# One transformer layer on one core: the last projection's first blocks by seven products, and the order around the second norm

## The chip, the cores and the metric

The program runs on one core of one Trainium2 chip. A core has four engines that this document speaks of: TensorE (PE, matrix products into eight banks of PSUM of 128 x 512 words each), VectorE (DVE), ScalarE (ACT) and SyncE (SP, which here issues loads and stores). Each takes its instructions in its own fixed order and waits on semaphores for the others. The metric is the device time of one launch in microseconds (us), smaller is better. Batch is 1, 512 tokens (S), model width 1024 (D), FFN width 2816, all in float32.

## The reference

The layer mixes the tokens in three branches, merges them and ends with a gated FFN. Only the end matters here; everything ahead of it is unchanged.

```python
    x = x + rms_norm(merged @ w_o, g_post_mix)

    hf = rms_norm(x, g_pre_ffn)
    f_gate, f_up = jnp.split(hf @ w_ffn_in, 2, axis=-1)
    f = (jax.nn.silu(f_gate) * f_up) @ w_ffn_out
    return x + rms_norm(f, g_post_ffn)
```

The last line but one's product with w_ffn_out (2816 x 1024) is the "last projection". The first two lines hold two norms: the one of merged @ w_o (its sum of squares is the first sum below) and the one of the new x (the second sum); the normed rows are then transposed to feed the FFN.

## The kernel before, in words

**Two halves of a number.** A product of two float32 matrices is made from three products of float32r operands: each operand is split into a high part (ScalarE copies it, line L119) and a low part (VectorE subtracts, L124), and TensorE adds high x high, high x low and low x high. So every operand costs ScalarE and VectorE one pass each, and each product block three matmuls. `split` at L118 does it.

**Weights.** A table `wlist` (L129 to L170) names every 128 x 1024 piece of weights in the order of its use. `unit()` hands out the next one and sees to it by `wload` that the two behind it are loaded by SP into one of two buffers `raw` and split into one of three buffers `hi` and `lo`. A tag in the table sends a unit's halves to a buffer of another pool (named u), which is how more of them can lie ready at the kernel's end.

**The two norms (`wo_norm`, L1039).** The 512 tokens are four blocks of 128, done as two pairs: `wo_norm(0)` and, later, `wo_norm(2)`, the "second norm" of this document. For each of four 128 x 512 half rows ScalarE squares with a sum (junk, L1047) and VectorE multiplies with the gain (yg, L1049). Then VectorE adds the sums (ss, L1051), makes an inverse root in twelve steps on 128 x 2 words (L273 to L279), updates x in four operations (xr, L1058), for which ScalarE squares again (L1060); a second sum (L1062) and inverse root, four multiplications (xn, L1070); TensorE transposes each in four pieces (tr, L1075); ScalarE copies (xf, L1081) and both split into fh and fl.

**The FFN's head (`ffn_head`, L1108).** The first three pairs of row blocks (six units of w_ffn_in, gate and up) run on all 512 tokens by plain products: `passes` (L221), first the six units over the first 256 tokens (fh, fl of `wo_norm(0)`), 144 matmuls of 128x256, then the same units over the others. `wo_norm(2)` runs beside them: its steps are handed out between matmuls, and a number of empty steps (L1064) sets before which matmul of the head its transposes stand. Behind it `begin_pairs` (L1154) prepares the first pair of the next stage: sums of token blocks (`make`), their splits (`halve`), and `pair_prep` (L1214 on), which sums and splits weight blocks.

**The pairs (`pairs`, L1248).** The other 19 of the 22 row blocks of gate and up go by seven products instead of eight (a 2 x 2 block scheme; product names s1 to s4, a11, a12, a22; `product` is L1250 with its matmul at L1254, z, y, r1 to r3 are its banks and partial results, rawp the raw weights of two buffers). Each product is 12 matmuls of 128x256. The result, silu(gate) x up, is stored as 22 slabs f of 128 x 512.

**The last projection (`down`, L1307).** It takes f by 11 units (pairs of row blocks, 256 rows of w_ffn_out by 512 columns each, per column half). `down(0, 0)` makes the first 512 columns of all tokens in four banks, one per token block, then `down(1, 4)` the others: `block` (L1322) does 6 matmuls of 128x512 at L1328. f is split (`f_split`, L1099) as the units of the first half come. `close` squares a bank with a sum and multiplies by the gain; with both halves' sums it makes the root, scales, adds x and stores. Units of the second half's last four are kept together, so that the four token blocks end one after the other and only the last is closed behind the last matmul.

The order of work is that of the code as written, except that a scheduler may exchange independent instructions between engines' queues, and `tc.issue_after(X)` keeps an instruction behind X in the order without a wait.

## Time and profile before

| what | value |
|---|---|
| median of 3 runs (lowest, highest) | 1130.61 us (1129.9, 1132.03) |
| the profiled execution's own time | 1130.71 us |
| its span (first to last instruction) | 1129.0 us |
| TensorE, share of the span | 99%, 6212 matmuls |
| VectorE, ScalarE | 70%, 53% |
| granted TensorE clock, mean | 0.999 |
| span of the FFN's head (771.43 to 811.14) | 39.71 us |
| span of the pairs (811.14 to 1000.33) | 189.19 us |
| last projection to the last matmul (1000.33 to 1121.79) | 121.46 us |
| behind the last matmul | 7.21 us |

The times in the trace count from the start of the span. The profiled execution is one launch; its own time is 0.10 us over the median. Busy times of matmuls overlap, since the next one starts before the last has ended; "x4" behind an operation of a timeline means four of them drawn together as one row. A bracket at the end of a timeline row is the idle time ahead of it and what ended it.

### The profile page before, as it was taken

The numbers are of one execution on the slowest core, as the hardware profiler recorded it, in microseconds if no ns is written. First come the engines' busy times: TensorE is split into PE (matmuls) and PEld (weight loads), VectorE is DVE, ScalarE is ACT, GpSimd is POOL, SyncE is SP. The second block draws the span as 40 slices with busy tenths as digits, with TensorE's granted clock in tenths as the row PEclk, the third lists the DMA queues.
The fourth block names the chain that finished last, engine by engine and source line by source line (L and its number), as shares of the span: only waits on it lengthen the run. The fifth ranks groups of instructions, "written<-read, shape, count | busy, mean of one in ns | idle before, by whom it ended". The sixth has DMA issues, their size and how long they took to land.

```text
span 1129.0 us, 15949 instructions
## 1 busy us (share of the span) xinstructions
PE 1117.4 (99%) x6212; PEld 965.6 (86%) x6212; DVE 790.4 (70%) x1425; ACT 599.1 (53%) x1077; POOL 23.2 (2%) x39
## 2 busy tenths in 40 slices
PE   9999999999999999999999999999999999999997
PEld 8888778888889888888888888888999999998886
DVE  6966967262675899999998644558887878882333
ACT  6757674132344786767776533334655555671221
POOL 1000202100000000000000000000000000000000
PEclk9999999999999999999999999999999999999999
DMA  8332325323232211111111252522233323323332
GB/s 307 111 93 75 112 94 204 95 75 102 84 94 76 75 38 56 38 57 57 38 58 56 74 204 94 150 85 65 75 112 110 101 90 113 113 94 98 107 94 75
DMA packets 29868, 108.74 MB, mean 96 GB/s; under 512 B 3232, under 2 KB 3520, under 8 KB 28640
## 3 DMA queue, kind: packets, MB, share of 16 engines
q1 hardware_dynamic: 27344, 97.98, 27.1%
q10 hardware_dynamic: 2160, 9.04, 2.2%
q8 instruction: 49, 0.80, 0.3%
q0 software_dynamic: 288, 0.69, 0.2%
q14 instruction: 27, 0.22, 0.1%
HBM read 105.60 MB, written 2.10 MB: 95 GB/s over the span
## 4 chain that ended last, share of the span: by engine, by line
PE 94%; DVE 3%; ACT 1%; DMA 1%; issue 0%; DVEq 0%; ACTq 0%
PE mm L221 42%; PE mm L1254 17%; PE mm L1328 11%; PE mm L507 4%; PE o L857 4%; PE mm L1032 3%; PE sc L819 3%; PE tr L844 3%; PE mm L735 2%; PE tr L651 1%; PE tr L433 1%; DMA rawp<-in_w_fi 1%; PE tr L567 1%; PE tr L757 1%; DVE lo L124 1%; PE mm L290 0%
## 5 line engine op out<-in xcount | busy, mean ns | idle before, releaser
L119 ACT ACTIVATE hi<-raw 128x1024 fp32r<-128x1024 f32 (+1 forms) x124 | 130.4, 1051 | 212.1 <-PE mm L221 86.2
L124 DVE TENSOR_TENSOR lo<-raw,hi 128x1024 fp32r<-128x1024 f32 (+1 forms) x124 | 151.4, 1221 | 128.5 <-ACT hi L119 121.4
L221 PE MATMUL mm<-hh,hi 128*128 128x512 f32 x504 | 199.9, 397 | 0.0
L221 PE MATMUL mm<-hh,lo 128*128 128x512 f32 x504 | 197.5, 392 | 0.2 <-DVE lo L124 0.2
L221 PE MATMUL mm<-hl,hi 128*128 128x512 f32 x504 | 197.2, 391 | 0.0
L221 PEld LDWEIGHTS mm<-hh,lo 128*128 128x128 f32 x504 | 94.6, 188 | 20.0 <-DVE lo L124 0.5
L221 PEld LDWEIGHTS mm<-hh,hi 128*128 128x128 f32 x504 | 94.7, 188 | 18.8 <-ACT hi L119 0.4
L221 PEld LDWEIGHTS mm<-hl,hi 128*128 128x128 f32 x504 | 94.7, 188 | 18.5 <-issue 0.2
L825 ACT ACTIVATE P<-P,ast 128x128 f32<-128x128 f32 (+3 forms) x128 | 70.6, 554 | 23.1 <-DVE ast L823 22.5
L1328 PE MATMUL mm<-hi,fs 128*128 128x512 f32 x256 | 79.8, 389 | 0.0
L823 DVE CUSTOM_DVE_ANT_0 P<-sc,mask 128x128 f32<-128x128 f32 (+3 forms) x128 | 57.9, 484 | 8.2 <-PE sc L819 7.3
L119 ACT ACTIVATE ph<-tr 128x512 fp32r<-128x512 f32 x80 | 47.0, 593 | 29.2 <-PE tr L844 28.3
L124 DVE TENSOR_TENSOR pl<-tr,ph 128x512 fp32r<-128x512 f32 x80 | 54.3, 684 | 5.1 <-ACT ph L119 3.2
L1328 PEld LDWEIGHTS mm<-hi,fs 128*128 128x128 f32 x256 | 48.1, 188 | 10.0
L819 PE MATMUL sc<-K,q 128*128 128x512 f32 (+2 forms) x192 | 50.9, 367 | 0.0
L1328 PE MATMUL mm<-lo,fs 128*128 128x512 f32 x128 | 49.8, 389 | 0.0
L1254 PE MATMUL mm<-t,hi 128*128 128x256 f32 x264 | 48.9, 283 | 0.0
L844 PE MATMUL tr<-ident,P 128*128 128x128 f32 x320 | 48.7, 273 | 0.0
L844 PEld LDWEIGHTS tr<-ident,P 128*128 128x128 f32 x320 | 39.1, 140 | 9.8 <-DVE pl L124 0.9
L1254 PEld LDWEIGHTS mm<-t,hi 128*128 128x128 f32 x264 | 41.1, 192 | 0.0
L1254 PE MATMUL mm<-fh,u 128*128 128x256 f32 x192 | 38.5, 283 | 0.0
L1254 PE MATMUL mm<-t,u 128*128 128x256 f32 x288 | 38.4, 283 | 0.0
(355 smaller groups left out, 2596.6 us busy)
## 6 DMA issues: line engine op xcount, KB each, us to landing
raw<-in_w_in SPq DMA_DIRECT2D x64, 512.0 KB, 3.6
rawp<-in_w_fi SPq DMA_DIRECT2D x19, 1024.0 KB, 5.0
raw<-in_w_br SPq DMA_DIRECT2D x24, 512.0 KB, 3.5
raw<-in_w_fo SPq DMA_DIRECT2D x22, 512.0 KB, 3.6
w<-in_cw ACTq DMA_DIRECT2D x4, 1024.0 KB, 6.8
raw<-in_w_o SPq DMA_DIRECT2D x8, 512.0 KB, 3.6
raw<-in_w_v SPq DMA_DIRECT2D x7, 512.0 KB, 5.1
raw<-in_w_fi SPq DMA_DIRECT2D x6, 512.0 KB, 3.6
```

What stands on the lines that cost most here:

```text
L119: SC.activation(hi, src, AF.Copy)
L124: res["lo"] = V.tensor_sub(lo, src, f32(hi))
L221: res["mm"] = PE.matmul(ps[:m, n0:n1], w[:, k * 128:k * 128 + m], x[k][:, n0:n1], start=(t == 0), stop=(t == 3 * NK - 1))
L507: res["mm"] = PE.matmul(b[c], x[k][:, c * 128:(c + 1) * 128], w[:, kk * 512:kk * 512 + 512], start=(k == 0 and t == 0), stop=(k == NK - 1 ...
L819: PE.matmul(ps[:, :w * n].rearrange("p (b n) -> p b n", b=w), lhs, K[:, i, brs[0]:brs[-1] + 1, :n], start=(i == 0), stop=(i == 1))
L823: V.tensor_tensor_reduce(out=t, in0=ps[:, b * n:b * n + n], in1=mask[0][:, S - n:], scale=-0.125, scalar=3.0e38, op0=OP.add, op1=OP.min, a ...
L825: SC.activation(t, t, AF.Exp, scale=-1.0, bias=st[:, 0, j, b:b + 1], accum_out=st[:, 1, j, b:b + 1])
L844: PE.transpose(pt[:, j * 128:(j + 1) * 128], self.part(j, br)[:, kt * 128:(kt + 1) * 128], ident)
L857: PE.matmul(po, VV[:, kt, g % 2, br].rearrange("p i d -> p (i d)"), x, start=(br == 0 and kt == 0 and t == 0), stop=(br == 1 and kt == a a ...
L1032: res["mm"] = PE.matmul(b[c, f], x[k][:, q], w[:, fs], start=(k == 0 and t == 0), stop=(k == NK - 1 and t == 2))
L1254: PE.matmul(ps, w[:, k * 128:k * 128 + 128], x[:, k], start=(start and k == t == 0), stop=(k == 3 and t == 2), skip_group_check=True)
L1328: PE.matmul(b[c], x[k][:, q], w[:, ws], start=(k == 0 and t == 0), stop=(k == NFF - 1 and t == 2))
```

## The change

**Last projection.** The first 4 of the 11 pairs of row blocks are multiplied in another way. Within two pairs of row blocks (one slab f of four row blocks), the operands are cut in 2 x 2: A by token half (256 tokens) and by even or odd row block, B by even or odd row block and by column half. The eight block products of such a matrix product are replaced by seven (1 to 7) of sums and differences: s1 to s4 of A (on VectorE, in the place of f), t1 to t4 of B (on VectorE, in the place of the loaded weights bs). Both slabs (q = 0, 1) go into the same banks, so a product is two halves of 12 matmuls, 128x512 each. `prep` splits the two operands of one half, A into one of four half buffers of u (which the pairs stage uses up to its end), B into the hi and lo buffers of the units. The other 7 pairs stay plain: `plain` is four `block`s. All eight banks hold partial results: w, x, y, z are two each. They are copied (s1, s5, early) or added between products, and `close` adds the copy first, where it has one (s). The raw weights of the four pairs are now loaded by four loads of 1 MB, whole slabs bs.

**Second norm.** The squares at L1047 are issued behind fh's last split of the first norm (`fhi`); the empty steps ahead of the transposes are 12 instead of 14; the steps of `begin_pairs` are issued behind xr (the first) or xn (the others) instead of yg.

```diff
-    HEAD, LAST, LASTV = 3, 4, 2
+    HEAD, LASTV = 3, 2
...
-    wlist += [(A["w_fo"][i], "y" if 22 - LAST <= i < 20 else None) for i in range(22)]
+    NS, NP = 4, NFF // 2
+    fo = {}
+    wlist += [(A["w_fo"][NP + i], None) for i in range(NS, 2 * NS)]
+    for n in (1, 2, 5, 6, 3, 7, 4):
+        if n == 4:
+            wlist.append((A["w_fo"][NP + 2 * NS], None))
+        wlist += [((n, q), None) for q in range(2)]
...
+            if isinstance(ap, tuple):
+                hi = wts.tile([128, 1024], F32R, tag="hi", name=nm("hi"), bufs=3)
+                lo = wts.tile([128, 1024], F32R, tag="lo", name=nm("lo"), bufs=3)
+                fo["prep"](*ap, hi, lo)
...
-                SC.activation(j, b[c, f], AF.Square, scale=0.5, accum_out=ss[:, f, c:c + 1])
+                with tc.issue_after(res["fhi"].ins) if "fhi" in res else nullcontext():
+                    SC.activation(j, b[c, f], AF.Square, scale=0.5, accum_out=ss[:, f, c:c + 1])
...
-        for _ in range({0: 8, 2: 14}[c0]):
+        for _ in range({0: 8, 2: 12}[c0]):
...
-        def step():
-            with tc.issue_after(res["yg"].ins):
+        def step(ins=res["xn"].ins):
+            with tc.issue_after(ins), tc.issue_after(res["fhi"].ins):
                 next(prep)
-        step()
+        step(res["xr"].ins)
...
+        misc = slab("misc", tag="y", shape=(2, 2, S))
+        fo["bs"] = [[slab("bs", tag="mo", shape=(2, 2, S)) for _ in range(2)] for _ in range(2)]
+        for h in range(2):
+            for q in range(2):
+                SY.dma_start(fo["bs"][h][q].rearrange("p u k n -> p u (k n)"),
+                             A["w_fo"][NP * h + 2 * q:NP * h + 2 * q + 2].rearrange("u p n -> p u n"))
...
+        def prep(n, q, hi, lo):
+            a, b = {1: ("a11", "b11"), 2: ("a12", "b21"), 5: ("s1", "b11"), 6: ("a11", "b11"), 3: ("a12", "b22"),
+                    7: ("a21", "b12"), 4: ("a22", "b21")}[n]
+            e = fo["n"] % 4
+            fo["n"] += 1
+            u = ff["unit"][e // 2][:, e % 2].rearrange("p (l i t) -> p l i t", l=2, i=2)
+            fo["a"][n, q] = u[:, 0], u[:, 1]
+            split(fo[a, q], u[:, 0], u[:, 1])
+            split(fo[b, q], *(t.rearrange("p (i n) -> p i n", i=2) for t in (hi, lo)))
...
+                d, x, y, op = {"s1": ("s1", "a21", "a22", OP.add), "s3": ("a21", "a11", "a21", OP.subtract),
+                               "s2": ("a11", "s1", "a11", OP.subtract), "s4": ("a12", "a12", "a11", OP.subtract),
+                               "t1": ("b11", "b12", "b11", OP.subtract), "t2": ("b11", "b22", "b11", OP.subtract),
+                               "t3": ("b12", "b22", "b12", OP.subtract), "t4": ("b21", "b21", "b11", OP.subtract)}[name[:2]]
+                V.tensor_tensor(g(d), g(x), g(y), op=op)
...
+        def product(n, q):
+            ps = {1: z, 6: z, 7: z, 4: z, 2: y, 5: w, 3: w}[n]
+            bh, bl = unit()
+            ah, al = fo["a"].pop((n, q))
+            for i in range(2):
+                f = slice(512 * i, 512 * i + 512)
+                for m in range(2):
+                    t = slice(128 * m, 128 * m + 128)
+                    mac(ps[m], (ah[:, i, t], bh[:, f]), (ah[:, i, t], bl[:, f]), (al[:, i, t], bh[:, f]))
...
+            ps, s = {(0, 0): (y, s1), (0, 1): (w, fo["early"]), (1, 0): (z, None), (1, 1): (x, s5)}[c // 2, h]
...
+        plain(1, NS)
...
+        plain(1, NS + 3)
+        fo_sum("s21", "t10")
+        product(1, 0)
+        fo_sum("t11")
+        product(1, 1)
+        for m in range(2):
+            SC.activation(fo["early"][m], w[m], AF.Copy)
+            begun.discard(id(w[m]))
+        product(2, 0)
+        product(2, 1)
...
+        for i in range(NS, NS + 3):
+            plain(0, i)
+        us = [unit() for _ in range(4)]
+        for c in range(4):
+            for i in range(4):
+                block(0, c, NS + 3 + i, *us[i])
+            close(0, c)
...
-    run([down(0, 0), down(1, LAST)])
+    down()
```

Left out are the buffers' tags, the rest of the products' order (2, 5, 6, 3, 7, a plain unit, 4, two plain units, the closing of the second column half), and the renaming of y in `close`.

What this does to the order of the instructions is shown at three places. **ScalarE at the second norm**, before: xf and fh are the last copies and splits of the first norm, junk at L1047 the squares of the second, a22h and hi belong to the preparation of the pairs.

```order
L1081 ACTIVATE xf_1128_6604<-tr_1132_6632 128x4x128 [waits PE_49]
L119 ACTIVATE fh_1016_5837<-xf_1128_6604 128x4x128 [waits Activation_49]
L1047 ACTIVATE junk_1138_6674,ss_5836<-mm_1105_6462 128x512 [waits PE_49]
L119 ACTIVATE a22h_1197_7023<-rawp_1160_6765 128x512 [waits DMAHW0_49]
L1081 ACTIVATE xf_1128_6604<-tr_1134_6648 128x4x128 [waits PE_49]
L1047 ACTIVATE junk_1140_6678,ss_5836<-mm_1106_6463 128x512 [waits DVE_49]
L119 ACTIVATE fh_1017_5838<-xf_1128_6604 128x4x128 [waits Activation_49]
L1047 ACTIVATE junk_1142_6682,ss_5836<-mm_1107_6464 128x512 [waits DVE_49,PE_49]
L1047 ACTIVATE junk_1144_6686,ss_5836<-mm_1108_6465 128x512 [waits DVE_49,PE_49]
L119 ACTIVATE hi_1189_6974<-rawp_1160_6765 128x1024 [waits DVE_49]
```

And after (the line numbers are those of the changed kernel; L1099 is the copy xf, L1065 the first squares, L1078 the second):

```order
L1099 ACTIVATE xf_1128_6604<-tr_1132_6632 128x4x128 [waits PE_49]
L119 ACTIVATE fh_1016_5837<-xf_1128_6604 128x4x128 [waits Activation_49]
L1099 ACTIVATE xf_1128_6604<-tr_1134_6648 128x4x128 [waits PE_49]
L119 ACTIVATE fh_1017_5838<-xf_1128_6604 128x4x128 [waits Activation_49]
L1065 ACTIVATE junk_1138_6674,ss_5836<-mm_1105_6462 128x512
L119 ACTIVATE a22h_1196_7008<-rawp_1160_6765 128x512 [waits DMAHW0_49]
L1065 ACTIVATE junk_1140_6678,ss_5836<-mm_1106_6463 128x512 [waits DVE_49]
L1065 ACTIVATE junk_1142_6682,ss_5836<-mm_1107_6464 128x512 [waits DVE_49,PE_49]
L1065 ACTIVATE junk_1144_6686,ss_5836<-mm_1108_6465 128x512 [waits PE_49,Activation_49]
L1078 ACTIVATE junk_1149_6719,ss_5836<-xr_1015_5833 128x512 [waits DVE_49,Activation_49]
L1078 ACTIVATE junk_1150_6722,ss_5836<-xr_1015_5833 128x512 [waits DVE_49,Activation_49]
```

The last xf and fh of the first norm have moved ahead of all four squares, and the split hi behind the second squares.

**VectorE at the second norm**, before: ss is the first sum of squares, the lines L273 to L279 the inverse root, xr the update that follows it; s13, a22l, rawp and lo belong to the preparation of the pairs.

```order
L1051 TENSOR_TENSOR ss_5836<-ss_5836 128x2
L1231 TENSOR_TENSOR s13_1195_6982<-rawp_1160_6765 128x1024 [waits DMAHW0_49,DVE_49]
L273 TENSOR_SCALAR rs_a_1146_6697<-ss_5836 128x2 [waits DVE_49]
L124 TENSOR_TENSOR a22l_1198_7024<-rawp_1160_6765,a22h_1197_7023 128x512
L274 TENSOR_SCALAR rs_i_1147_6698<-rs_a_1146_6697 128x2 [waits DVE_49]
L1239 TENSOR_TENSOR rawp_1160_6765<-s13_1195_6982,rawp_1160_6765 128x512
L275 TENSOR_SCALAR ss_5836<-rs_i_1147_6698 128x2 [waits DVE_49]
L1241 TENSOR_TENSOR rawp_1160_6765<-rawp_1160_6765 128x512 [waits DVE_49]
L277 TENSOR_TENSOR rs_t_1148_6699<-ss_5836 128x2 [waits DVE_49]
```

And after, up to the first update of x and behind the four of them:

```order
L1069 TENSOR_TENSOR ss_5836<-ss_5836 128x2
L289 TENSOR_SCALAR rs_a_1146_6697<-ss_5836 128x2 [waits DVE_49]
L290 TENSOR_SCALAR rs_i_1147_6698<-rs_a_1146_6697 128x2 [waits DVE_49]
L291 TENSOR_SCALAR ss_5836<-rs_i_1147_6698 128x2 [waits DVE_49]
L293 TENSOR_TENSOR rs_t_1148_6699<-ss_5836 128x2 [waits DVE_49]
```

```order
L295 SCALAR_TENSOR_TENSOR ss_5836<-rs_t_1148_6699,ss_5836 128x2 [waits DVE_49]
L1076 SCALAR_TENSOR_TENSOR xr_1015_5833<-yg_1139_6676,ss_5836,xr_1015_5833 128x512 [waits DVE_49]
L1076 SCALAR_TENSOR_TENSOR xr_1015_5833<-yg_1141_6680,ss_5836,xr_1015_5833 128x512
L1076 SCALAR_TENSOR_TENSOR xr_1015_5833<-yg_1143_6684,ss_5836,xr_1015_5833 128x512
L1076 SCALAR_TENSOR_TENSOR xr_1015_5833<-yg_1145_6688,ss_5836,xr_1015_5833 128x512
L1249 TENSOR_TENSOR s13_1195_6970<-rawp_1160_6765 128x1024 [waits DMAHW0_49]
```

No operation of the preparation is left in the inverse root; the subtraction s13 stands behind the four updates.

**TensorE at the first transposes of the second norm**, before: mm_1175 is the bank of the head's sixth unit (hi_1166), tr the transposes of xn.

```order
L221 MATMUL mm_1169_6847<-fh_1017_5838,lo_1163_6788 128x256
L221 MATMUL mm_1175_6893<-fh_1016_5837,hi_1166_6818 128x256 [waits DVE_49]
L221 MATMUL mm_1175_6893<-fl_1018_5839,hi_1166_6818 128x256
L221 MATMUL mm_1175_6893<-fh_1016_5837,lo_1167_6819 128x256
L221 MATMUL mm_1175_6893<-fh_1016_5837,hi_1166_6818 128x256
L221 MATMUL mm_1175_6893<-fl_1018_5839,hi_1166_6818 128x256
L1075 MATMUL tr_1171_6862<-ident_99,xn_1170_6860 128x128 [waits DVE_49,PE_49]
L1075 MATMUL tr_1171_6862<-ident_99,xn_1170_6860 128x128 x3
```

And after, where mm_1172 is the bank of the fifth unit (hi_1162):

```order
L237 MATMUL mm_1172_6858<-fl_1018_5839,hi_1162_6787 128x256
L237 MATMUL mm_1172_6858<-fh_1016_5837,lo_1163_6788 128x256
L237 MATMUL mm_1172_6858<-fh_1016_5837,hi_1162_6787 128x256
L237 MATMUL mm_1172_6858<-fl_1018_5839,hi_1162_6787 128x256
L1093 MATMUL tr_1170_6849<-ident_99,xn_1169_6847 128x128 [waits DVE_49,PE_49]
L1093 MATMUL tr_1170_6849<-ident_99,xn_1169_6847 128x128 x3
```

The first transposes stood behind 125 matmuls of the head and stand now behind 104.

**ScalarE where the pairs end and the last projection begins**, after: u_1187 is a buffer of the pairs stage, filled here for product 2; r1, r2 and r3 are copies that free banks of the last pair, fs splits of f.

```order
L119 ACTIVATE fs_1409_9628<-f_1188_6961 128x512 [waits DVE_49]
L1278 ACTIVATE r2_1346_9139<-mm_1339_9042 128x256 [waits PE_49]
L119 ACTIVATE fs_1409_9628<-f_1188_6961 128x512
L119 ACTIVATE u_1187_6960<-f_1159_6764 128x512 [waits PE_49]
L1298 ACTIVATE r1_1349_9156<-mm_1347_9154 128x256 [waits PE_49]
L119 ACTIVATE u_1187_6960<-f_1222_7393 128x512
L119 ACTIVATE hi_1374_9304<-raw_1373_9302 128x1024 [waits DMAHW5_49,PE_49]
L119 ACTIVATE fs_1388_9415<-f_1185_6958 128x512 [waits PE_49]
```

Before, the copy of r1 from mm_1347 stood behind splits fs only, and u was filled (with splits of f) behind the split of a unit:

```order
L119 ACTIVATE fs_1389_9480<-f_1185_6970 128x512 [waits DVE_49]
L119 ACTIVATE fs_1389_9480<-f_1185_6970 128x512
L1280 ACTIVATE r1_1349_9156<-mm_1347_9154 128x256 [waits PE_49]
L119 ACTIVATE fs_1371_9307<-f_1222_7393 128x512 x2
L119 ACTIVATE hi_1369_9303<-raw_1368_9301 128x1024 [waits DMAHW5_49,PE_49]
L119 ACTIVATE u_1187_6972<-f_1185_6970 128x512 x2
L119 ACTIVATE u_1186_6971<-f_1255_7846 128x512 [waits PE_49]
```

The split into u_1187, which waits for TensorE, has moved ahead of the copy r1.

## Rows read from the trace of the kernel before

**Rows 1.** The page: engines (part 1), chain (4), a matmul group (5), a load (6)

```profile
PE 1117.4 (99%) x6212; PEld 965.6 (86%) x6212; DVE 790.4 (70%) x1425; ACT 599.1 (53%) x1077; POOL 23.2 (2%) x39
...
PE 94%; DVE 3%; ACT 1%; DMA 1%; issue 0%; DVEq 0%; ACTq 0%
...
L1328 PE MATMUL mm<-hi,fs 128*128 128x512 f32 x256 | 79.8, 389 | 0.0
...
rawp<-in_w_fi SPq DMA_DIRECT2D x19, 1024.0 KB, 5.0
```

**Rows 2.** Table by stages: stretch, length, busy of each engine (count), clock, DMA

```profile
771.43:811.14 39.71, 37.69 (x307) 36.66 (x306) 32.62 (x61) 21.48 (x37) 0.00 (x0) 1.00 0.15 54
811.14:1000.33 189.19, 189.19 (x1584) 189.19 (x1584) 154.77 (x193) 112.86 (x196) 0.00 (x0) 1.00 0.30 101
1000.33:1121.79 121.46, 121.44 (x542) 100.24 (x540) 44.74 (x67) 34.85 (x53) 0.00 (x0) 1.00 0.30 96
```

**Rows 3.** Chain that ended last, in order of time: start, length, piece

```profile
1003.63 118.16 PE mm L1328 x521
```

**Rows 4.** Timeline of VectorE, then ScalarE, 988 to 1016: start, length, operation

```profile
990.33 2.36 DVE L124 TENSOR_TENSOR lo<-raw,hi 128x1024 fp32r<-128x1024 f32 x2
...
1006.63 2.49 DVE L124 TENSOR_TENSOR fs<-f,fs 128x512 fp32r<-128x512 f32 x4
...
1003.95 2.18 ACT L119 ACTIVATE fs<-f 128x512 fp32r<-128x512 f32 x4
...
1007.57 1.06 ACT L119 ACTIVATE hi<-raw 128x1024 fp32r<-128x1024 f32 x1 [0.92 <-PE mm L1328]
```

**Rows 5.** Timeline of TensorE, 992 to 1004.5

```profile
994.58 1.60 PE L1254 MATMUL mm<-t,u 128*128 128x256 f32 x12
...
998.77 0.28 PE L1254 MATMUL mm<-fh,u 128*128 128x256 f32 x1
...
1003.47 0.40 PE L1328 MATMUL mm<-lo,fs 128*128 128x512 f32 x1
```

**Rows 6.** Timeline of TensorE, three stretches between 771.4 and 794.6

```profile
772.75 0.28 PE L221 MATMUL mm<-fh,u 128*128 128x256 f32 x1
773.80 0.50 PE L221 MATMUL mm<-fh,u 128*128 128x256 f32 x2 [0.77 <-ACT fh L119]
774.61 0.39 PE L221 MATMUL mm<-fl,u 128*128 128x256 f32 x1 [0.30 <-DVE fl L124]
...
787.90 0.28 PE L221 MATMUL mm<-fl,hi 128*128 128x256 f32 x1
788.71 0.63 PE L1075 MATMUL tr<-ident,xn 128*128 128x128 f32 x4 [0.53 <-DVE xn L1070]
...
792.32 0.60 PE L1075 MATMUL tr<-ident,xn 128*128 128x128 f32 x4
...
794.30 0.39 PE L221 MATMUL mm<-fl,u 128*128 128x256 f32 x1 [0.34 <-DVE fl L124]
```

**Rows 7.** Timeline of VectorE from 748 and from 769, then of ScalarE

```profile
749.04 0.15 DVE L1051 TENSOR_TENSOR ss<-ss 128x2 f32<-128x2 f32 x1
...
751.60 0.75 DVE L1058 SCALAR_TENSOR_TENSOR xr<-yg,ss,xr 128x512 f32<-128x512 f32 x1
...
775.67 0.15 DVE L1051 TENSOR_TENSOR ss<-ss 128x2 f32<-128x2 f32 x1
775.74 1.22 DVE L1231 TENSOR_TENSOR s<-rawp 128x1024 f32<-128x1024 f32 x1
...
781.71 2.74 DVE L1058 SCALAR_TENSOR_TENSOR xr<-yg,ss,xr 128x512 f32<-128x512 f32 x4
785.24 0.16 DVE L1062 TENSOR_TENSOR ss<-ss 128x2 f32<-128x2 f32 x1 [0.79 <-ACT junk L1060]
...
787.81 2.74 DVE L1070 SCALAR_TENSOR_TENSOR xn<-xr,ss,gb 128x512 f32<-128x512 f32 x4
...
770.54 0.58 ACT L1047 ACTIVATE junk<-mm 128x512 f32<-128x512 f32 x1
```

More of the change, by code (lines that the diff above doesn't have):

```diff
@@ L1 @@
-from contextlib import ExitStack
+from contextlib import ExitStack, nullcontext
 import concourse.bass as bass
@@ new lines, in down, with mac, block @@
+    def down():
+        w, x, z, y = ([bank(t) for _ in range(2)] for t in ("tr", "mm", "mm", "mm"))
+        s1, s5 = [row("s1", tag="tg") for _ in range(2)], [row("s5", tag="q32") for _ in range(2)]
+        begun = set()
+        res["gf"] = [row("gf") for _ in range(2)]
+        for i in range(2):
+            SC.dma_start(res["gf"][i], bass.AP(tensor=A["grow"].tensor, offset=A["grow"].offset + 2 * D + 512 * i,
+                                               ap=[[0, 128], [1, 512]]))
+            V.tensor_scalar(res["gf"][i], res["gf"][i], -0.5, None, op0=OP.mult)
+        with tc.issue_after(res["silu"].ins):
+            SC.activation(warm, warm, AF.Sqrt)
+        def mac(ps, *ops):
+            for i, (a, b) in enumerate(ops):
+                PE.matmul(ps, a, b, start=id(ps) not in begun, stop=i == len(ops) - 1, skip_group_check=True)
+                begun.add(id(ps))
+        def block(h, c, i, hi, lo):
+            ps = {(0, 0): y, (0, 1): w, (1, 0): z, (1, 1): x}[c // 2, h][c % 2]
@@ L1333, in close, with plain @@
+        def plain(h, i):
+            u = unit()
+            for c in range(4):
+                block(h, c, i, *u)
+        def close(h, c):
             ss = res["ss"]
-            y = res["y"].t[f][:, c, :]
+            if "y" not in res:
+                res["y"] = Pair("yo", tag="mo")
+            yo = res["y"].t[h][:, c, :]
+            ps, s = {(0, 0): (y, s1), (0, 1): (w, fo["early"]), (1, 0): (z, None), (1, 1): (x, s5)}[c // 2, h]
             j = row("junk")
-            SC.activation(j, b[c], AF.Square, accum_out=ss[:, f, c:c + 1])
@@ L1357, in ahead @@
-        def ahead(i):
-            if f == 0 and i < n:
-                f_split(2 * i)
-                f_split(2 * i + 1)
-        ahead(1)
-        for i in range(n - last):
-            hi, lo = unit()
-            ahead(i + 2)
-            for c in range(4):
-                block(c, i, hi, lo)
-                yield
-        us = [unit() for _ in range(last)]
-        for c in range(4):
-            for i in range(last):
-                block(c, n - last + i, *us[i])
-                yield
-            close(c)
+                V.scalar_tensor_tensor(yo, yo, r, res["x"][c][:, fs], op0=OP.mult, op1=OP.add)
@@ new lines, in down @@
+        product(2, 0)
+        product(2, 1)
+        fo_sum("t20")
+        for m in range(2):
+            SC.activation(s1[m], z[m], AF.Copy)
+        product(5, 0)
+        fo_sum("t21")
+        product(5, 1)
+        fo_sum("s4")
+        product(6, 0)
+        product(6, 1)
+        fo_sum("t30")
+        for m in range(2):
+            SC.activation(s5[m], w[m], AF.Copy)
+        product(3, 0)
+        fo_sum("t31")
+        f_split(8)
+        product(3, 1)
+        for m in range(2):
+            V.tensor_add(fo["early"][m], z[m], fo["early"][m])
@@ new lines, in down @@
+        fo_sum("t40")
+        product(7, 0)
+        fo_sum("t41")
+        product(7, 1)
+        plain(1, 8)
+        for m in range(2):
+            V.tensor_add(s5[m], z[m], s5[m])
+        f_split(9)
+        product(4, 0)
+        product(4, 1)
+        f_split(10)
+        plain(1, 9)
+        plain(1, 10)
+        for c in range(4):
+            close(1, c)
+        for i in range(NS, NS + 3):
+            plain(0, i)
+        us = [unit() for _ in range(4)]
+        for c in range(4):
+            for i in range(4):
+                block(0, c, NS + 3 + i, *us[i])
+            close(0, c)
```

107 lines of the change are left out of this document (63 added, 44 removed).

## The prediction

> **What bounds the kernel now.** I read the page first: TensorE is busy 99% of the span [rows 1], at the full granted clock (PEclk 1.00) in all these stages [rows 2], and the chain that ended last is TensorE for 94% [rows 1]. So a microsecond of its work is worth a microsecond as long as the other engines deliver in time, and idle time of VectorE (70%) or ScalarE (53%) is worth nothing. Then the table by stages, cut at the places that the change touches [rows 2]: the first projection's tail and the head of the FFN (771.43 to 811.14), the pairs (811.14 to 1000.33, no idle TensorE), the last projection (1000.33 to 1121.79, 0.02 us idle), and behind its end a tail of 1129.0 - 1121.79 = 7.21 us without TensorE. So there are two sources of time: matmuls of the last projection, and some 2 us of idle TensorE in the FFN's head.
>
> What a matmul costs is read from the pace, not from its busy time. The page's row of the group says 389 ns for one 128x512 matmul [rows 1]; but in the chain 521 of them take 118.16 us [rows 3], 0.2268 us each, since each starts before the one ahead has ended. With 128x256 operands the pace is 189.19/1584 = 0.1194 us [rows 2]. Here the two ways of reading differ in the sum: the Trainium skill (Perfetto Trace Analysis, Identifying the Most-Contended Engine) calls the busy share of matmuls no good measure of how near to the limit TensorE is, because matmuls are pipelined. By busy time the change's 24 matmuls would be 24 x 0.389 = 9.3 us, by pace 5.4. The chain bears the page out; the higher figure is kept below as a rival.
>
> **Seven products instead of eight.** Before, the last projection is 11 units x 2 column halves x 4 token blocks x 6 = 528 matmuls. Four of the 11 pairs are 192 of them; after, 7 products x 2 halves x 12 = 168, all of the same 128x512 shape with a 128x128 weight load each. So 24 go: 24 x 0.2268 = **5.44 us** on the path, if nothing new makes TensorE wait. The tail is not touched: the last block to be closed adds nothing to its bank (its list entry is None), so squares, root, two multiplications and output keep the 7.21 us.
>
> What the change adds lies on VectorE and ScalarE. Per product half: the split of a 128x512 activation block and of a 128x1024 weight block, where a plain unit has one weight split per 5.44 us. Then 8 activation sums (0.6 us), 8 weight sums (1.14), a few copies and additions of banks. These follow each other every 0.60 us (512) and 1.14 us (1024) on VectorE, on ScalarE every 0.54 us (512; 1.06 for one of 1024) [rows 4]. From the end of the first product to the end of the seventh's second half, 12 halves, TensorE has 12 x 2.72 = 32.7 us; VectorE's order holds there 15 operations of 1024 and 14 of 512: 17.1 + 8.4 = 25.5 us, 78%. So it fits on average. Does it fit in order? A weight half is prepared three ahead (three hi and lo buffers): ScalarE waits until the half three back is read. Today ScalarE starts 0.24 us after such an end: 17 matmuls of the unit are left at 1003.47 [rows 5], so at the pace it ends at 1007.33, and the next split starts at 1007.57 [rows 4]. Of all halves the tightest is the first of product 6. Counted from the end of product 1, ScalarE needs 0.24 to see it, 0.54 each for the copy of a z bank and an activation block, 1.06 for the weight block; then VectorE 1.22 for the low half and 1.14 for the sum t2: 4.7 us, which is 2.0 after the end of product 2's first half. There follow in VectorE's order an activation low half 0.6, a weight low half 1.14, the sum t4 1.14, the second t2 1.14 and product 6's own low half 1.22: done at 7.3 us. TensorE comes to it three halves after that end, at 8.2 us. So 0.9 us is left there, elsewhere 1.2 to 8. Operations with strided sources are not dearer: the subtraction L1231, over two separated halves of a pair's slab, takes 1.22 us [rows 7] as the plain one does. I take 0 us for waits in the products. From above: if it is short by 0.5 us at each of the six tightest halves, +3.
>
> The four bank pairs z, w, x, y are all eight banks. Where a bank is read before the next product goes on, work for other banks stands between: after product 1, z is copied while products 2 and 5 run (10.9 us for 2 x 0.54); before product 7, z is added by VectorE during product 3. Cost 0; if a read were late, each such place costs up to the 0.6 to 0.7 us of one read.
>
> One step may not be free at the join. On ScalarE the split for product 2 now stands ahead of the copy that frees the last pair's bank, and it waits for TensorE. It overwrites the first half of a buffer, which the s2 product reads (done at 996.2), not the second half, which s4 reads until 999.05 [rows 5]. The copy is wanted when the next product starts, at 998.89 (0.12 after the row of 998.77). The split waits and takes 0.54, the copy behind it some 0.37 with its release. Behind s2: 996.2 + 0.54 + 0.37 = 997.1, early enough, 0 us. Behind the whole buffer: 999.1 + 0.54 + 0.37 = 1000.0, 1.1 us late. I take 0, since the two halves are separate columns, and keep 1.1.
>
> The loads: SP now holds four 1 MB loads behind the fourth unit's; they wait for pair buffers that are free at 1003.5 at the latest [rows 5], and with 5.0 us to landing [rows 1] are there at some 1010; the first use is at 1014 or later. Loads behind them in the queue are wanted after 1050. Cost 0.
>
> **The second norm.** In the FFN's head TensorE loses time at five places, start to start less the pace of 0.12 us [rows 6]: 772.75 to 773.80 is 0.93 too long (it waits for fh), two matmuls to 774.61 are 0.57 (fl), 787.90 to 788.71 is 0.69 (xn, before the first transposes), and from 792.32 to 794.30, four transposes of 0.095 and six matmuls, 0.88 (fh and fl again); 3.07 in all. The change puts ScalarE's squares behind the last fh. Then xf starts at 770.54 in the first square's place [rows 7], fh at 771.15, done at 771.78; fl at 772.5; TensorE wants them at 772.87 and 772.99. So the first two, 1.50 us, vanish.
>
> The rest hangs on VectorE's chain. The squares end about when they do today (a22h 0.54 from 771.69, then four of 0.6 to 0.7: 774.8), and VectorE's sum ss, which today comes at 775.67 [rows 7], stays near 775.55. But today five large operations of the pair preparation sit in the inverse root, 6.04 us from ss to xr; the earlier norm without them takes 2.56 [rows 7]. The change's order puts them behind: xr at 778.1. From xr to the second sum it is 3.53 today; one 1.14 us subtraction now stands there, so 3.8; from it to xn 2.57, from xn to the transposes 0.90 [rows 6, 7]. First transposes at 778.1 + 3.8 + 2.57 + 0.90 = 785.35, 3.36 earlier than the 788.71 of today. Against this: they now stand behind 104 matmuls of the head, not 125, so 21 x 0.12 = 2.53 more are left behind them. Net 0.83, and the late fl waits go from 0.88 to about 0.6 (VectorE again: four fl with the moved preparation in between, the last done at 793.9 where TensorE wants it at 793.3). **1.1 us gained.** TensorE will still wait, for 1.35 us, at the first transposes. Bounds: all of the losses go, 3.1 gained; or the chain is no earlier than now, and the 21 matmuls come behind it, 2.5 lost. I take 1.1, since 2.56 and 6.04 are both from rows of the same twelve steps. The pairs behind have no idle time to give back [rows 2], so the gain is kept.
>
> **Sum.** Against the profiled execution (1130.71 us, of which 1129.0 are the span, and 0.10 above the median of the three runs): 1130.61 - 5.44 - 1.1 = **1124.1 us** as a median, 0.6% faster.
>
> **Rivals.**
> 1. The norm's chain is not earlier, since VectorE takes the moved operations at another place or ScalarE's squares run later: TensorE waits at the transposes with 21 matmuls behind them. 1130.6 - 5.4 + 2.5 = 1127.7. For it: TensorE's own position moved more than two steps of the loop. Against: the order has no large operation left in the first inverse root.
> 2. The three weight buffers become the limit and the kernel is slower. Mechanism: a half starts only when ScalarE has got its buffer back and VectorE has finished the low half. Three halves then take 2.72 + C, with C the time from release to ready; TensorE's pace needs C up to 5.44. I get at most 4.6. To be 2.3 us slower than today all 14 halves must lose 6.5 + 2.3 = 8.8 us, in 14/3 periods 1.9 each, so C = 7.3. That wants VectorE and ScalarE 1.6 times as slow as their rows, or two further sums before each split. Time then 1133 and more. Short of this, C at 6 costs 2.6: 1126.7.
> 3. The join waits for the whole buffer: 1125.2.
> 4. The busy time counts, 9.3 instead of 5.4: 1120.2. Against it is the chain's pace.
> 5. That the change doesn't remove the matmuls is excluded by the order, which has 24 fewer on TensorE.
>
> **How the numbers follow.** Two runs of this kernel tell 0.2% (2.3 us) from no change. Forecast with its bounds (1122.1 to 1126, rival 3 within it) 0.79; rival 1 0.07; the buffers with a partial loss, 1126 to 1130, 0.06; slower by rival 2, 0.04; rival 4 0.04. The range goes from 1130.6 - 5.4 - 3.1 = 1122.1 to 1126.8: the norm's gain lost and rival 3's 1.1 with 0.5 for a tight half. Faster by over 0.2% (below 1128.3): 0.79 + 0.07 + 0.04 and a third of 0.06, 0.92; slower 0.04; the same 0.04.
>
> **What would show it.** Last projection: TensorE's stage 5.4 us shorter (116.0 us from its first matmul to its last), 504 matmuls at 0.2268 with no wait for lo or hi over 0.1 us; one wait at the first half of product 6 would be the first sign of rival 2. FFN's head: no wait for fh near 773, one of some 1.3 us for xn near 784, head ending near 810.0. The join: no gap before the s3 product at 998.9 - 1.1 = 997.8. The forecast is wrong if the pace in the products is over 0.23, if the pairs show idle TensorE, or if the tail is not 7.2.

## The result, and the profile after

| | median of the runs | profiled run | its span |
|---|---|---|---|
| before | 1129.91 us (6 runs, 1129.14 to 1132.03) | 1130.71 us | 1129.0 us |
| changed | 1123.37 us (6 runs, 1122.38 to 1124.78) | 1122.85 us | 1121.1 us |

The ratio of the runs is 0.9936, 95% interval 0.9926 to 0.9946, which is 6.1 to 8.4 us less; the two medians lie 6.5 us apart, where 6.54 = 5.44 + 1.1 was forecast. (The forecast stood on 1130.61 for before, the median of three runs.) The two profiled runs are 7.9 us apart: the one of before lies 0.8 above its median and the changed one 0.5 below, and the stages below account for all of it.

The page of the changed kernel, parts 1, 4 and 6, beside [rows 1]:

```profile
PE 1110.2 (99%) x6188; PEld 960.3 (86%) x6188; DVE 821.6 (73%) x1463; ACT 611.8 (55%) x1095; POOL 24.1 (2%) x39
...
PE 92%; DVE 4%; ACT 2%; DMA 1%; issue 0%; DVEq 0%; ACTq 0%
...
bs<-in_w_fo SPq DMA_DIRECT2D x4, 1024.0 KB, 7.3
```

VectorE has gone from 70% to 73%, the chain is still TensorE. The table by stages (stretch, length, busy of PE, PEld, DVE, ACT, POOL with counts, clock, DMA share, GB/s), beside [rows 2]: the FFN's head, the pairs, the last projection to the last matmul, the tail, and products 1 to 7 (the six that run in a row):

```profile
771.38:809.48 38.10, 36.85 (x307) 36.48 (x306) 32.97 (x61) 21.34 (x39) 0.00 (x0) 1.00 0.17 56
809.48:998.68 189.20, 189.20 (x1585) 189.20 (x1585) 155.09 (x193) 113.35 (x196) 0.00 (x0) 1.00 0.32 110
998.68:1114.55 115.87, 115.86 (x518) 95.81 (x516) 75.17 (x105) 46.90 (x70) 0.00 (x0) 1.00 0.26 86
1114.55:1121.10 6.55, 0.00 (x0) 0.00 (x0) 2.80 (x8) 0.98 (x3) 0.00 (x0) 0.75 0.23 80
1022.06:1054.70 32.64, 32.64 (x145) 27.03 (x145) 27.89 (x31) 20.93 (x28) 0.00 (x0) 1.00 0.05 15
```

The head is 1.61 us shorter, the pairs are the same to 0.01, the last projection is 5.59 shorter and TensorE waits 0.01 us in it.

The tail is 6.55 where it was 7.21. From the last matmul to the end of the last multiplication both have 3.7 us, and the last store lands 5.7 us behind the last matmul in both. The difference comes behind that, in the waits with which SyncE ends the program: it goes through the semaphores of the transfers one after the other, in the same order in both kernels. Before, the last three stores have the third to fifth of its nine waits, and four more, 0.6 us, follow the last store; in the changed kernel they have the last three, and none follows. This is not chance between runs: all ten traces with the products have a tail of 6.6 us, both without them 7.2. It fits the last projection's loads, 18 where there were 22, which would move the later transfers on to other semaphores; no run tests that.

In the chain of the changed kernel, beside [rows 3], each product takes 24 matmuls at 5.44 us, and the last 180 matmuls 40.81:

```profile
1032.94 5.44 PE tr L1388 x24
1038.38 5.44 PE mm L1388 x24
...
1073.74 40.81 PE mm L1388 x180
```

That is 0.2267 us for one, and 0.2268 before.

### The profile page after: what moved, and what is told of

The parts are those of the page before. It is cut to its first block, busy times and chain, and to the rows that moved or that the text cites. A ratio compares the mean times of both kernels' runs of the same rounds, so it can differ in the third digit from the quotient of the medians.

```text
span 1121.1 us, 15955 instructions
## 1 busy us (share of the span) xinstructions
PE 1110.2 (99%) x6188; PEld 960.3 (86%) x6188; DVE 821.6 (73%) x1463; ACT 611.8 (55%) x1095; POOL 24.1 (2%) x39
## 4 chain that ended last, share of the span: by engine, by line
PE 92%; DVE 4%; ACT 2%; DMA 1%; issue 0%; DVEq 0%; ACTq 0%
PE mm L237 42%; PE mm L1272 17%; PE mm L1388 8%; PE mm L523 4%; PE o L873 4%; PE sc L835 3%; PE tr L860 3%; PE tr L1388 3%; PE mm L751 2%; PE mm L1048 2%; PE tr L667 1%; PE tr L449 1%; DMA raw<-in_w_fi 1%; PE tr L583 1%; PE tr L773 1%
## 5 line engine op out<-in xcount | busy, mean ns | idle before, releaser
L119 ACT ACTIVATE hi<-raw 128x1024 fp32r<-128x1024 f32 (+1 forms) x116 | 121.9, 1051 | 170.7 <-PE mm L237 81.3
L124 DVE TENSOR_TENSOR lo<-raw,hi 128x1024 fp32r<-128x1024 f32 (+1 forms) x116 | 141.7, 1222 | 89.8 <-ACT hi L119 82.7
L1388 PE MATMUL mm<-hi,fs 128*128 128x512 f32 x136 | 43.7, 389 | 0.0
L835 PEld LDWEIGHTS sc<-K,q 128*128 128x128 f32 x192 | 32.4, 189 | 6.7 <-DVE ast L839 0.9
L1272 PE MATMUL mm<-fh,hi 128*128 128x256 f32 x132 | 37.4, 283 | 0.0
```

What stands on the lines that cost most here:

```text
L119: res["hi"] = SC.activation(hi, src, AF.Copy)
L124: res["lo"] = V.tensor_sub(lo, src, f32(hi))
L835: PE.matmul(ps[:, :w * n].rearrange("p (b n) -> p b n", b=w), lhs, K[:, i, brs[0]:brs[-1] + 1, :n], start=(i == 0), stop=(i == 1))
L1272: PE.matmul(ps, w[:, k * 128:k * 128 + 128], x[:, k], start=(start and k == t == 0), stop=(k == 3 and t == 2), skip_group_check=True)
L1388: PE.matmul(ps, a, b, start=id(ps) not in begun, stop=i == len(ops) - 1, skip_group_check=True)
```

## The experiments

Intervals are at 95%. "Head" below is the time from the start of the pass ahead of the FFN's head (168 matmuls at 725 to 727) to the first matmul of the pairs: 85.28 us before, 83.89 in the changed kernel. It is longer than the stage of the table by that pass. "Stage" is the head of the table alone, from its own first matmul on: 39.71 before, 38.10 changed. The pass by itself takes 45.40 to 45.96 us over the twelve traces, mostly by a wait ahead of the first norm's transposes near 767: 0.34 us in the changed kernel's trace, 0.12 in that of before, none in the other ten, whatever the edit. So the stage is the better measure: in five traces with the changed kernel's order it is 38.02 to 38.13 us, where the head is 83.26 to 83.89.

**The two parts apart.** First the products with the norm's order of before; then the kernel before with the norm's order changed.

```diff
 # e1: on the changed kernel (the preparation's first step loses its argument, too)
-                with tc.issue_after(res["fhi"].ins) if "fhi" in res else nullcontext():
-                    SC.activation(j, b[c, f], AF.Square, ...)
+                SC.activation(j, b[c, f], AF.Square, ...)
...
-        for _ in range({0: 8, 2: 12}[c0]):
+        for _ in range({0: 8, 2: 14}[c0]):
...
-            with tc.issue_after(ins), tc.issue_after(res["fhi"].ins):
+            with tc.issue_after(res["yg"].ins):
 # e2: the same lines the other way, on the kernel before
```

> The seven products stay, the order around the second norm is the one of before (transposes behind 125 matmuls of the head, preparation of the pairs behind yg, squares not moved). Theory: the two parts of the change add, and the products bring 24 matmuls at 0.2268 = 5.4 us: about 1124.5 beside 1129.9 of before, ratio 0.995; FFN's head as long as before (39.7 us), last projection 115.9 us, no wait of TensorE in it. Rival (busy time counts): 9.3 us, ratio 0.992. Rival (the products lose some of it to waits and the norm's order brings the rest): last projection over 117 us, ratio 0.997 or more.

> The kernel before with only the order around the second norm changed. Theory: 1.1 us by the prediction, 1.6 by the head's length in the trace of the changed kernel (38.10 for 39.71): ratio 0.9986 to 0.9990; first transposes of the second norm near 785.0, behind 104 matmuls; last projection 121.5 us as before. Rival (the gain there depends on the products or is given back in the pairs): ratio 1.000, with idle time of TensorE in the pairs.

Measured: products alone 1124.21 us, ratio 0.9949 (0.9936 to 0.9961), 5.8 us less by the medians; norm alone 1129.04, ratio 0.9990 (0.9981 to 0.9999), 1.0 us less. Together 6.8, within the 6.1 to 8.4 of the whole change; the theory held in both. TensorE in the run with the products alone, at the head (the waits of [rows 6] are there again, as long), and its last projection, in which it is never idle:

```profile
773.54 0.50 PE L237 MATMUL mm<-fh,u 128*128 128x256 f32 x2 [0.75 <-ACT fh L119]
774.35 0.39 PE L237 MATMUL mm<-fl,u 128*128 128x256 f32 x1 [0.30 <-DVE fl L124]
...
788.46 0.63 PE L1092 MATMUL tr<-ident,xn 128*128 128x128 f32 x4 [0.54 <-DVE xn L1087]
...
1000.10:1115.90 115.80, 115.80 (x518) 95.83 (x516) 75.20 (x105) 46.89 (x70) 0.00 (x0) 1.00 0.26 88
```

From the first matmul of the pairs to the last of all it is 305.07 us there and in the changed kernel, 310.65 before and 310.62 with the norm alone. So 5.58 us belong to the products, 0.14 more than 24 matmuls by pace; this 0.14 I can't place. With the 0.6 us of the tail the products bring 6.2 us in the traces. By busy time (9.3) the matmuls would have brought over 60% more. The stage is 39.69 us with the products alone and 38.13 with the norm alone, as before and as changed: the parts add, and nothing is given back.

**What of the norm's order counts.** One piece at a time undone in the changed kernel: the pairs' preparation back behind yg; ScalarE's squares no longer held.

```diff
 # e3
-        def step(ins=res["xn"].ins):
-            with tc.issue_after(ins), tc.issue_after(res["fhi"].ins):
+        def step():
+            with tc.issue_after(res["yg"].ins):
...
-        step(res["xr"].ins)
+        step()
 # e4
-                with tc.issue_after(res["fhi"].ins) if "fhi" in res else nullcontext():
-                    SC.activation(j, b[c, f], AF.Square, ...)
+                SC.activation(j, b[c, f], AF.Square, ...)
```

> The changed kernel, but the steps of the pairs' preparation are issued behind yg again, so that five large operations sit in the inverse root. In the order the first transposes then stand behind 128 matmuls. Theory: the time from ss to xr goes from 2.56 back to 6.0 us, the first transposes from 785.0 to about 788.7, and with 24 matmuls fewer behind them the head ends near 810.8 where it ended at 809.5: about 1.3 us slower than the changed kernel, ratio to before 0.9952 to 0.9955. Rival (the prediction's lower bound, 21 matmuls behind a chain that is no earlier): 3.5 us slower than the changed kernel, ratio 0.997.

> The changed kernel, but ScalarE's four squares are not held behind the last split of the first norm; they go where the scheduler puts them. By the prediction's sum the two waits near 773 come back, 0.93 + 0.57 = 1.5 us: ratio to before about 0.995. Rival: VectorE's chain, not these waits, sets when the first transposes run; then TensorE waits 1.5 us at 773 and as much less at the transposes (1.0 there today), and the head ends within 0.5 us of 809.5: ratio 0.9935 to 0.9940.

Measured: preparation back 1124.47 us, ratio 0.9950 (0.9938 to 0.9963), head 85.06, stage 39.78; squares back 1122.61, ratio 0.9937 (0.9923 to 0.9950), head 83.60, stage 38.26. The first has the whole loss of the old order again: TensorE at the first transposes, and VectorE's ss and xr, 6.05 us apart:

```profile
788.84 0.63 PE L1093 MATMUL tr<-ident,xn 128*128 128x128 f32 x4 [1.25 <-DVE xn L1088]
...
775.79 0.15 DVE L1069 TENSOR_TENSOR ss<-ss 128x2 f32<-128x2 f32 x1
...
781.84 2.74 DVE L1076 SCALAR_TENSOR_TENSOR xr<-yg,ss,xr 128x512 f32<-128x512 f32 x4
```

The second loses 0.1 to 0.2 us of the stage and nothing that the times show. TensorE waits for fh near 773 again, though for less than before; it then waits less, and earlier, at the transposes, since VectorE's chain starts earlier, too:

```profile
772.60 0.51 PE L237 MATMUL mm<-fh,u 128*128 128x256 f32 x2 [0.40 <-ACT fh L119]
...
783.67 0.66 PE L1092 MATMUL tr<-ident,xn 128*128 128x128 f32 x4 [0.41 <-DVE xn L1087]
...
773.86 0.15 DVE L1068 TENSOR_TENSOR ss<-ss 128x2 f32<-128x2 f32 x1
```

The head's first matmul is at 770.61 here and at 771.38 in the changed kernel; counted from it, the sum ss and the first transposes both come 0.6 us earlier, and the transposes stand behind 96 matmuls instead of 104. So the place of the five large operations of VectorE is the norm's gain. Holding the squares is worth next to nothing: it takes away a wait near 773 and makes the chain start later. What each of the two would cost alone, no run shows.

**How much room VectorE has in the products.** The low halves made again, with the same result: of the activation block once more, of the weight block once and twice more.

```diff
             split(fo[a, q], u[:, 0], u[:, 1])
+            V.tensor_sub(u[:, 1], fo[a, q], f32(u[:, 0]))            # e5
             split(fo[b, q], *(t.rearrange(...) for t in (hi, lo)))
+            h2, l2 = (t.rearrange(...) for t in (hi, lo))             # e6; twice in e7
+            V.tensor_sub(l2, fo[b, q], f32(h2))
```

> The changed kernel; VectorE makes the low half of each activation block of the products twice (0.6 us more in each of 14 halves, same result). Theory: the 12 middle halves then hold 25.5 + 7.2 = 32.7 us of VectorE's work in 32.7 us of TensorE's, and the spare time at the tightest half (0.9 us by the prediction, 2.0 in the trace of the changed kernel) covers what the order loses: 0 to 0.5 us slower, TensorE's first waits for lo at product 6 if any. Rival (no slack at all is used, VectorE is far from the limit): no wait at all, also 0. Rival (the buffers' cycle is already at its limit): 14/3 x 3 x 0.6 = 8 us slower.

> The changed kernel; VectorE makes the low half of each weight block of the products twice (1.14 us more in each of 14 halves, same result). Theory (VectorE's rate): 25.5 + 13.7 = 39.2 us of work in 32.7 of TensorE's; 6.5 less the slack of 2 to 3 us: 3 to 5 us slower than the changed kernel, with waits of TensorE for lo of about 1 us each from product 6 on. Rival (the cycle of three buffers, C from 4.6 to 5.7 against 5.44): 0.3 x 14/3 = 1.2 us slower.

> As the one with the weights' low half made twice, but three times (2.28 us more per half). Theory (VectorE's rate): 25.5 + 27.4 = 52.9 us in 32.7: 20.2 less 2 to 3 of slack, 17 to 19 us slower than the changed kernel, waits of TensorE in nearly every half. Rival (cycle of buffers, C = 6.9): 1.44 x 14/3 = 6.7 us slower.

Measured: 1123.07 us, ratio 0.9934 (0.9918 to 0.9950), no change; 1127.23, ratio 0.9972 (0.9962 to 0.9982), 3.9 us over the changed kernel's median; 1142.37, ratio 1.0107 (1.0093 to 1.0121), 19.0 over it. (In the two traces, from the first matmul of the pairs to the last of all, 5.3 and 21.6 more, a little over the 3 to 5 and 17 to 19 of the theory.) All three go with VectorE's rate and not with the buffers' cycle, by which they would be 8 (if it stood at its limit), 1.2 and 6.7 us slower; the last also holds time lost to the clock (last section). The products 1 to 7 with 0.6 us more per half:

```profile
1022.46:1055.10 32.64, 32.64 (x145) 27.03 (x145) 32.31 (x38) 19.90 (x26) 0.00 (x0) 1.00 0.03 6
```

VectorE is busy for 32.31 of 32.64 us, and TensorE still never waits. The Trainium skill (Perfetto Trace Analysis, Identifying the Most-Contended Engine) says that for VectorE, other than for TensorE, occupancy is a fair measure of how near it is to its limit; these runs agree, with no loss at 99% and a loss at the next larger load that was tried. With the weights' low half made twice, 1.14 us more, TensorE's waits and a stretch in which VectorE has no idle time (22.00 of 22.00):

```profile
1036.94 0.50 PE L1390 MATMUL tr<-lo,u 128*128 128x512 f32 x1 [0.99 <-DVE lo L1360]
...
1040.95 0.50 PE L1390 MATMUL mm<-lo,u 128*128 128x512 f32 x1 [0.75 <-DVE lo L1360]
...
1044.96 0.50 PE L1390 MATMUL mm<-lo,u 128*128 128x512 f32 x1 [0.54 <-DVE lo L1360]
...
1053.94 0.73 PE L1390 MATMUL tr<-hi,fs 128*128 128x512 f32 x2 [1.44 <-ACT hi L119]
...
1034.00:1056.00 22.00, 18.28 (x77) 13.84 (x76) 22.00 (x24) 11.44 (x15) 0.00 (x0) 1.00 0.00 0
```

The idle time in these waits comes to 3.72 us, but from the first matmul of the pairs to the last of all this trace has 310.34 us, 5.27 more than the changed kernel. A wait costs more than the idle time that is drawn: counted from start to start against 0.2268, the four cost 4.4 us, and the matmul behind each starts another 0.11 late. The loss of 3.9 by the medians is nearer to the idle time by chance. The first wait is at product 5's second half, not at product 6 as I had thought.

**Filling what is left.** TensorE still waits 1.04 us at the first transposes. Transposes later, and the preparation behind the last fl; then each alone.

```diff
 # e8: both; e9: the two tables alone; e10: fl2 and step alone
-        for _ in range({0: 8, 2: 12}[c0]):
+        for _ in range({0: 8, 2: 16}[c0]):
...
+                res["fl2"] = res["lo"]
-                for _ in range({0: 1, 2: 2}[c0]):
+                for _ in range({0: 1, 2: 1}[c0]):
...
-        def step(ins=res["xn"].ins):
-            with tc.issue_after(ins), tc.issue_after(res["fhi"].ins):
+        def step():
+            with tc.issue_after(res["fl2"].ins):
...
-        step(res["xr"].ins)
+        step()
```

> The changed kernel, with 16 empty steps instead of 12 ahead of the second norm's transposes and 1 instead of 2 between them (in the order: behind 120, 126, 132 and 138 matmuls instead of 104, 108, 120 and 132), and the steps of the pairs' preparation behind the last low half fl. Theory: the 1.04 us that TensorE waits at the first transposes is filled with 16 matmuls, and fl comes earlier without the preparation between: 1 to 1.7 us faster than the changed kernel, near 1122, head ending at 808 to 808.5. Rival (what is not waited for at the transposes is waited for at fl): head ends at 809.5 with a wait for fl of over 1 us, no gain.

> The changed kernel with only the 16 empty steps and 1 between the transposes (behind 120, 126, 132 and 138 matmuls as in the run with transposes later); the preparation of the pairs stays behind xr and xn. If the place of the transposes alone brought that run's 1.6 us, the head (from the start of the pass ahead of it to the pairs) is 82.3 us here too, 83.9 in the changed kernel. Rival: the preparation then stands between the copies and low halves that TensorE waits for, with fewer matmuls between: waits for fh and fl of 2 to 3 us where there is none at the transposes, head 84 us or more.

> The changed kernel with only the preparation of the pairs behind the last low half fl; 12 empty steps and 2 between, as changed (the scheduler puts the transposes behind 98, 108, 120 and 132 matmuls). Theory: the transposes wait for xn as before, 1 to 2 us, since VectorE's chain sets them; fl is no longer waited for, 0.2 us: head 83.5 to 84, time as the changed kernel within 0.5 us. Rival (the preparation between the low halves was what cost): head 82.3.

Measured: both 1121.80 us, ratio 0.9924 (0.9911 to 0.9937), head 82.30, stage 37.07; steps alone 1123.17, 0.9936 (0.9920 to 0.9953), head 84.25, stage 38.99; preparation alone 1123.20, 0.9943 (0.9928 to 0.9958), head 83.92, stage 38.58. With both, the view of waits lists none of TensorE's in the head, and the last two fl are made from 790.20 on; in the changed kernel TensorE waited for its last until 793.63:

```profile
785.38 0.60 PE L1093 MATMUL tr<-ident,xn 128*128 128x128 f32 x4
...
790.20 1.29 DVE L124 TENSOR_TENSOR fl<-xf,fh 128x512 fp32r<-128x512 f32 x2
```

With the steps alone the transposes are not waited for either, but fh and fl are, as that run's rival had it:

```profile
786.13 0.60 PE L1093 MATMUL tr<-ident,xn 128*128 128x128 f32 x4
...
792.33 0.74 PE L237 MATMUL mm<-fh,u 128*128 128x256 f32 x4 [1.44 <-ACT fh L119]
...
793.92 0.39 PE L237 MATMUL mm<-fl,u 128*128 128x256 f32 x1 [0.62 <-DVE fl L124]
```

With the preparation alone the transposes stand behind 98 matmuls and are waited for 1.36 us, as the chain decides:

```profile
784.59 0.63 PE L1093 MATMUL tr<-ident,xn 128*128 128x128 f32 x4 [1.36 <-DVE xn L1088]
```

Alone, the steps lengthen the stage by 0.9 us and the preparation by 0.5; together they shorten it by 1.0. (The heads differ by 1.6, but 0.56 of that is the pass.) The run with both is the fastest of all: 1.3 us under the run with the activation's low halves made twice, which shared its chip and runs of before and is as fast as the changed kernel. The intervals of the two ratios overlap, so against the changed kernel the times alone leave it likely, and the stages (37.07, against 38.02 to 38.13 in five traces with the changed kernel's order) show where it comes from.

## Why the prediction was right, point by point

**The sum.** Right in mechanism, but that the medians differ by just the 6.5 us forecast is luck. The traces add up to 7.8: 5.6 from the products' matmuls, 0.6 from the tail and 1.6 from the head's stage. The forecast had 5.44, nothing and 1.1.

**The tail.** The forecast named a tail other than 7.2 us among its signs of being wrong, and it is 6.6. Its reason, that the work behind the last matmul stays the same, is true up to the landing of the last store; the term that it put at nothing is the 0.6 us of SyncE's closing waits, which come in another place among the stores.

**Seven products.** Right: 24 matmuls at the pace, 5.44 forecast, 5.58 between the same two points of the traces. That nothing makes TensorE wait held too, but with two slips. The share of VectorE was named 78% for "12 halves from the end of the first product"; 12 halves run from its start, and by busy time the table above has 27.89 of 32.64 us, 85%. And the tightest half has more room than said. VectorE from the first t2 on, then ScalarE's copy of z and TensorE:

```profile
1030.22 1.23 DVE L1370 TENSOR_TENSOR bs<-bs,bs 128x1024 f32<-128x1024 f32 x1
...
1034.23 1.22 DVE L1370 TENSOR_TENSOR bs<-bs,bs 128x1024 f32<-128x1024 f32 x1
1035.37 1.22 DVE L124 TENSOR_TENSOR lo<-bs,hi 128x1024 fp32r<-128x1024 f32 x1
...
1026.86 0.60 ACT L1471 ACTIVATE s<-mm 128x512 f32<-128x512 f32 x1 [0.68 <-PE mm L1388]
...
1038.44 0.39 PE L1388 MATMUL mm<-lo,u 128*128 128x512 f32 x1
```

The last row is product 6's first matmul that reads its low half, at 1038.44; that low half is done at 1035.37 + 1.22 = 1036.59, so 1.9 us are left, not 0.9. The step that was too dear is the start of the chain: the copy of z at 1026.86 stands 0.6 us ahead of product 1's end (1027.50), since the first of the two banks is complete before the product is. The sum t2 starts at 1030.22, when product 2's first half ends, and is done 1.2 us behind it, not 2.0. The rest is as forecast: 1.14 us from one large operation to the next, on strided operands too.

**Rival 2** was rightly small, but its mechanism was the wrong one. What comes first when VectorE is loaded is its rate over all halves, not the cycle of three buffers; the 8.8 us that it needed would, as an estimate between the two last loads above, take some 1.5 us more of VectorE per half.

**The join and the loads.** Right. In the changed kernel the split u starts at 994.44, when the product that began at 992.92 has read its operands, the copy r1 at 994.97, and the next product 0.12 us behind the matmul ahead of it:

```profile
994.44 0.63 ACT L119 ACTIVATE u<-f 128x512 fp32r<-128x512 f32 x1
994.97 0.37 ACT L1298 ACTIVATE r<-mm 128x256 f32<-128x256 f32 x1
...
1011.22 1.06 ACT L119 ACTIVATE hi<-bs 128x1024 fp32r<-128x1024 f32 x1 [0.93 <-PE mm L1388]
...
992.92 1.60 PE L1272 MATMUL mm<-t,u 128*128 128x256 f32 x12
...
997.12 0.28 PE L1272 MATMUL mm<-fh,u 128*128 128x256 f32 x1
997.24 1.60 PE L1272 MATMUL mm<-t,u 128*128 128x256 f32 x12
```

The third ScalarE row is the first split of a 1 MB load: it waits for TensorE to give the buffer back, not for the load. These loads took 7.3 us to land (page, above), not 5.0; the slack took it. A run in which the split waits for the whole buffer was not made.

**The second norm.** Right in mechanism, too small in size: 1.1 us forecast, 1.6 by the stages (39.71 and 39.69 against 38.02 to 38.13). The time of the run alone, 1.0 us less with 0.1 to 2.1 as its interval, can't tell the two apart. TensorE at the transposes and at the last fl, then VectorE from ss to xn, beside [rows 6, 7]:

```profile
785.04 0.63 PE L1093 MATMUL tr<-ident,xn 128*128 128x128 f32 x4 [1.04 <-DVE xn L1088]
...
792.90 0.52 PE L237 MATMUL mm<-fh,u 128*128 128x256 f32 x3
793.63 0.39 PE L237 MATMUL mm<-fl,u 128*128 128x256 f32 x1 [0.21 <-DVE fl L124]
...
775.23 0.15 DVE L1069 TENSOR_TENSOR ss<-ss 128x2 f32<-128x2 f32 x1
...
777.79 2.74 DVE L1076 SCALAR_TENSOR_TENSOR xr<-yg,ss,xr 128x512 f32<-128x512 f32 x4
780.45 1.22 DVE L1249 TENSOR_TENSOR s<-rawp 128x1024 f32<-128x1024 f32 x1
781.59 0.15 DVE L1080 TENSOR_TENSOR ss<-ss 128x2 f32<-128x2 f32 x1
...
784.14 2.74 DVE L1088 SCALAR_TENSOR_TENSOR xn<-xr,ss,gb 128x512 f32<-128x512 f32 x4
```

Forecast and measured: ss to xr 2.56 and 2.56; xr to the second sum 3.8 and 3.80; to xn 2.57 and 2.55; to the transposes 0.90 and 0.90; the wait there 1.35 and 1.04. Two terms make the missing 0.5. The sum ss comes at 775.23 instead of 775.55, so the transposes come 0.3 earlier than forecast; and the late fl, forecast at 0.6 from start to start, costs 0.37 (792.90 to 793.63 less three matmuls). The step "the first two, 1.50 us, vanish" is true of the trace and worth next to nothing by the run with the squares back. It did no harm, since the sum was made from the transposes and not from the waits that go.

**Rival 1's price** was wrong: 2.5 us lost with the chain unmoved. With the preparation back the head is as before and not longer (85.06), since the scheduler then puts the transposes behind 128 matmuls by itself. How many matmuls stand ahead of them is not set by the number of empty steps alone, and the bound of "21 matmuls behind a late chain" could not occur in this way.

## What to carry to other kernels

Where one engine is the bound, cost a removed instruction by its pace in the chain, and look at the others by two numbers: their busy share in the stretch, and the time from each operand being ready to its first use. Sum a moved stall at the last event of its chain, not over the waits that go: the two waits near 773, which went ahead of a later one, brought no more than some 0.2 us here. When an engine waits at one point, filling that wait only pays if what comes behind it is early too: both edits of the last experiment were needed. Count a wait from start to start, and compare stages that begin behind the noise of the one ahead. And look at the end of the program when the number of transfers changes: which semaphores the last stores have was worth 0.6 us here.

## What was not expected of the hardware

With the weights' low halves made three times, TensorE waits up to 2.5 us at a time, and behind the three waits of 2.1 to 2.5 us its granted clock falls from 2.4 to 1.2 GHz. Two stretches of the table, and some rows of the timeline behind one wait:

```profile
1050.00:1060.00 10.00, 9.13 (x32) 6.38 (x30) 10.00 (x12) 3.69 (x5) 0.00 (x0) 0.83 0.00 0
1060.00:1070.00 10.00, 6.64 (x18) 4.71 (x18) 10.00 (x11) 2.62 (x4) 0.00 (x0) 0.69 0.00 0
...
1038.76 0.50 PE L1391 MATMUL tr<-lo,u 128*128 128x512 f32 x1 [2.34 <-DVE lo L1361]
...
1041.46 0.63 PE L1391 MATMUL tr<-lo,u 128*128 128x512 f32 x1
1041.89 1.48 PE L1391 MATMUL tr<-hi,u 128*128 128x512 f32 x3
1043.17 0.43 PE L1391 MATMUL tr<-lo,u 128*128 128x512 f32 x1
1043.43 0.39 PE L1391 MATMUL tr<-hi,u 128*128 128x512 f32 x1
```

In the stretch from 1060 the mean granted clock is 0.69. Behind the wait of 2.34 us the four matmuls from 1041.46 on start every 0.43 us, nearly twice 0.2268; the one at 1043.17 is followed after 0.26. With waits of 0.5 to 1.4 us, in the run with twice, the clock stays at 1.00. So a wait of TensorE can cost more than its own length in this way, too. How much of the 19.0 us this is can't be told from here, since VectorE was busy without a break (10.00 of 10.00) in the same stretches and a faster TensorE would have waited for it.
